# Moving the weight sums and the gate-times-up products of a Strassen-Winograd SwiGLU from GpSimd to VectorE

## The chip, the cores and the metric

The kernel runs on one core of one Trainium2 chip. The metric is the device time of one execution in microseconds (us). Five instruction engines take part: TensorE (PE: matmuls, with its weight loads shown as PEld), VectorE (DVE), ScalarE (ACT), GpSimd (POOL) and the SP queue, which only issues DMAs. Each engine runs its own instructions in their order; semaphores tie the engines to each other.

## The reference

One decoder layer in float32 over 1024 tokens and 1024 channels. The part that matters here is its feed-forward block, with 2816 hidden columns:

```python
n2 = rms_norm(h, g_ffn[i])
h = h + (jax.nn.silu(n2 @ w_ffn_gate[i]) * (n2 @ w_ffn_up[i])) @ w_ffn_down[i]
```

Ahead of it stand the two attention branches and their merge, behind it a gated per-layer embedding and the last RMSNorm.

## The kernel before

Each float32 factor of a matmul is split in two parts: `split` (lines 128 to 130) lets ScalarE cast it to the high part (L129) and VectorE subtract that from the source to get the low part (L130). `passes` (L132 to L137) then does three matmuls for each pair of blocks: high by high (L135), high by low of the moving operand (L136), low by high (L137). So the first two matmuls of a group wait for ScalarE only, and the third is the first that needs VectorE's low part.

The gate and up matmuls are done in **units**: 22 of them, alternately 256 columns of `w_ffn_gate` and the same 256 of `w_ffn_up`; two such units are called a pair. A unit's 1 MB of weights (tile `raw`, three buffers) comes by a DMA on the SP queue (L860). In `wino` a unit is a two-by-two block product done with seven products in place of eight (the Strassen-Winograd scheme). Each product is twelve matmuls of 128x512. Its left factor is a quarter of the weights or a sum of quarters, split into a tile `wl` with three buffers, so that ScalarE and VectorE prepare a product while TensorE is up to two products behind. The sums of quarters are four instructions of 128x512 for each unit on GpSimd: `s1` (L989) and L990 as soon as the weights are there, L1006 behind product 1, L1008 behind product 2.

The seven products have the order 1, 5, 2, 6, 7, 3, 4, and units overlap: products 1 and 5 of a unit, then 3 and 4 of the unit before it, then 2, 6 and 7 of the unit. The products' results are combined on VectorE by `add` (L999), three for each unit. A gate unit passes its four results through SiLU on ScalarE (L1035). An up unit multiplies its four results by those of the gate unit (`ready`, L1051): three on GpSimd (L1054), the last, straight from the bank, on VectorE (L1056). From these it forms the sums for the down matmul on VectorE (L1047) and stores all to DRAM on the SP queue (L1044). Between the units VectorE also forms sums of the down weights (`down_sums`, L1140).

The engines' instruction orders aren't written by hand: a scheduler takes the program and lays out each queue by its own estimate of times. Ahead of the units, VectorE normalizes the hidden state (L875) with a scale that TensorE broadcasts into the bank `bc` (L764) and forms the right factors `b`.

Of the kernel before, what the change touches and what calls it, by code (L numbers as in the profile page):

```python
# [14 lines left out]
ALU = mybir.AluOpType  # L15
# [36 lines left out]
def decoder_layer(ctx: ExitStack, tc: tile.TileContext, x, p, positions, g_mix, w_in, g_q_a, w_q_b,  # L52
                  g_kv_a, w_kv_b, w_br_mla, w_br_sb, w_out, g_ffn, w_ffn_gate, w_ffn_up, w_ffn_down,
                  w_ple_gate, w_ple_proj, g_ple, g_final, xT, pT, out):
    nc = tc.nc
# [72 lines left out]
    def split(h, l, src, eng=nc.vector):  # L128
        nc.scalar.copy(out=h, in_=src)  # L129
        eng.tensor_tensor(out=l, in0=src, in1=r32(h), op=ALU.subtract)  # L130

    def passes(ps, prods, first=True, last=True, **kw):  # L132
        n = len(prods)
        for i, ((ah, al), (bh, bl)) in enumerate(prods):
            nc.tensor.matmul(ps, lhsT=ah, rhs=bh, start=first and i == 0, stop=False, **kw)  # L135
            nc.tensor.matmul(ps, lhsT=ah, rhs=bl, start=False, stop=False, **kw)  # L136
            nc.tensor.matmul(ps, lhsT=al, rhs=bh, start=False, stop=last and i == n - 1, **kw)  # L137
# [17 lines left out]
    with ExitStack() as att:  # L155
# [17 lines left out]
        with ExitStack() as sb:  # L173
# [306 lines left out]
            for pr in range(HEADS // 2):  # L480
                kst, q1, q2 = cur
                oT = wp.tile([P, S], F32, name="oT", tag="oT", bufs=1)
                for a in range(2):
# [5 lines left out]
                                            op=ALU.subtract)  # L489
# [365 lines left out]
    def t_tile():  # L855
        return wk.tile([P, HALF], F32, name="t", tag="t", bufs=16)
# [127 lines left out]
    def wino(raw, order, ctile, ready):  # L984

        a11, a12, a21, a22 = [raw[:, kh * 4:kh * 4 + 4, f * P:(f + 1) * P] for f in range(2) for kh in range(2)]
        s1 = wk.tile([P, 4, P], F32, name="s1", tag="c", bufs=4)
        G = nc.gpsimd
        G.tensor_tensor(out=s1, in0=a21, in1=a22, op=ALU.add)  # L989
        G.tensor_tensor(out=a21, in0=a11, in1=a21, op=ALU.subtract)  # L990
        left = {1: a11, 2: a12, 3: a12, 4: a22, 5: s1, 6: a11, 7: a21}
        bank, s = {}, {}

        def snap(key, pt):
            s[key] = ctile()
            nc.scalar.copy(out=s[key], in_=pt)

        def add(key, pt):
            latest["add"] = nc.vector.tensor_tensor(out=s[key], in0=pt, in1=s[key], op=ALU.add).ins  # L999
            return s[key]  # L1000

        for n, i in enumerate(order):
            w = wk.tile([P, 2, 4, P], F32R, name="wl", tag="wl", bufs=3)
            split(w[:, 0], w[:, 1], left[i])
            if i == 1:
                G.tensor_tensor(out=a11, in0=s1, in1=a11, op=ALU.subtract)  # L1006
            elif i == 2:
                G.tensor_tensor(out=a12, in0=a12, in1=a11, op=ALU.subtract)  # L1008
            k = "P" if i in (1, 6, 7, 4) else "R" if i == 2 else "Q"
            first = k not in bank  # L1010
            if first:
                spec = B if k == "R" else next(firsts) if k == "Q" and order is FIRST else A
                bank[k] = ps.tile([P, HALF], F32, name="p" + k, **spec)
            pt = bank[k]
            passes(pt, [((w[:, 0, kk, :], w[:, 1, kk, :]), (Bn[i][:, 0, kk, :], Bn[i][:, 1, kk, :]))
                        for kk in range(4)], first=first, last=i in (2, 3, 4), skip_group_check=True)
            if i in (1, 6):
                snap(i, pt)
            elif i == 2:
                ready(0, 0, add(1, pt))  # L1020
            elif i == 3:
                ready(0, 1, add(6, pt))
            elif i == 4:
                ready(1, 0, None, pt)
            elif (12 - i) in s:
                ready(1, 1, add(12 - i, pt))
            else:
                snap(i, pt)
            yield

    def gate_unit(raw, order, ctile, sl):
        def ready(f, t, c, pt=None):
            if c is None:
                c = t_tile()
            nc.scalar.activation(out=c, in_=c if pt is None else pt, func=AF.Silu)  # L1035
            sl[f, t] = c

        return wino(raw, order, ctile, ready)

    def up_unit(j, raw, order, ctile, sl):  # L1040
        done = {}

        def store(i, src):
            nc.sync.dma_start(out=d_g[(7 * j + i - 1) * P:(7 * j + i) * P, :], in_=src)  # L1044

        def sub(i, dst, a, b):
            nc.vector.tensor_tensor(out=dst, in0=a, in1=b, op=ALU.subtract)  # L1047
            done[i] = dst
            store(i, dst)

        def ready(f, t, u, pt=None):  # L1051
            g = sl[f, t]
            if pt is None:
                nc.gpsimd.tensor_tensor(out=g, in0=g, in1=u, op=ALU.mult)  # L1054
            else:
                nc.vector.tensor_tensor(out=g, in0=pt, in1=g, op=ALU.mult)  # L1056
            done[f, t] = g
            if (f, t) != (0, 1):
                store({(0, 0): 1, (1, 0): 2, (1, 1): 3}[f, t], g)
            if 7 not in done and (1, 1) in done and (0, 1) in done:  # L1060
                sub(7, t_tile(), done[1, 1], done[0, 1])
            if 5 not in done and 7 in done and (0, 0) in done:
                sub(5, done[0, 1], done[0, 1], done[0, 0])
                sub(6, t_tile(), done[1, 1], done[5])
            if 4 not in done and 6 in done and (1, 0) in done:
                sub(4, t_tile(), done[1, 0], done[6])

        return wino(raw, order, ctile, ready)
# [264 lines left out]
```

## Time and profile before

| | |
|---|---|
| median of 3 runs | 1748.95 us (1746.61 to 1750.78) |
| the profiled execution | 1749.03 us, of which the profiled span is 1747.2 us |
| TensorE busy | 1665.0 us (95%), mean granted clock 0.983 |
| VectorE busy | 1115.2 us (64%) |
| ScalarE busy | 881.3 us (50%) |
| GpSimd busy | 368.6 us (21%), 389 instructions |
| the stage of the units | about 993 to 1428 us of the span |

Times in the profile are microseconds from the start of the span. "Busy" is the time in which an engine executes; a matmul of 128x512 shows as some 0.39 us busy though the next one starts after some 0.23 us, since matmuls are pipelined. An idle time has behind it, in brackets, what ended it (the releaser).

### The profile page before, as it was taken

Reading aid. Unit: us, or ns where it says so; the run is one execution under the profiler, and the core shown is the slowest. Engines: PE = TensorE matmul, PEld = TensorE weight load, DVE = VectorE, ACT = ScalarE, POOL = GpSimd, SP = SyncE. Lnnn points to the kernel's source line nnn. Section 1 sums busy time; section 2 is a strip of 40 time slices with the busy share of each in tenths; the row PEclk is TensorE's granted clock in tenths of the full one; section 3 lists DMA queues with packets and bytes.
Section 4 is the critical chain, followed back from the end, with each engine's and each line's share of the span. In section 5 each row is a group of like instructions: output and inputs, shape, how many; then the busy total and the mean of one; then the engine's idle time right before and its main releaser. Section 6 shows DMA issues by size and latency. Waiting matters only on the chain.

```text
span 1747.2 us, 22835 instructions
## 1 busy us (share of the span) xinstructions
PE 1665.0 (95%) x8100; PEld 1383.4 (79%) x8100; DVE 1115.2 (64%) x1874; ACT 881.3 (50%) x1740; POOL 368.6 (21%) x389
## 2 busy tenths in 40 slices
PE   6999999999987999998999899999999999999997
PEld 5887778777776788886789787877778778888787
DVE  6655785576766777686568745565666545656665
ACT  5255676576675776686325633333333334445412
POOL 2012220000021333331001733344344310000000
PEclk9999999999998999999999999999999999999998
DMA  5221222212223322124854423364564528665522
GB/s 175 59 69 37 61 57 65 67 60 67 85 85 127 104 68 86 59 70 157 284 201 153 145 78 129 126 216 151 187 197 163 199 88 316 193 193 183 170 81 74
DMA packets 167987, 222.10 MB, mean 127 GB/s; under 512 B 22914, under 2 KB 97666, under 8 KB 167874
## 3 DMA queue, kind: packets, MB, share of 16 engines
q1 hardware_dynamic: 161298, 200.21, 35.6%
q0 software_dynamic: 6032, 19.93, 3.3%
q8 instruction: 63, 1.03, 0.2%
q10 hardware_dynamic: 544, 0.52, 0.1%
q14 instruction: 50, 0.41, 0.1%
HBM read 151.93 MB, written 67.90 MB: 126 GB/s over the span
## 4 chain that ended last, share of the span: by engine, by line
PE 74%; DVE 10%; issue 6%; ACT 4%; DMA 3%; POOL 3%; SPq 0%; POOLq 0%; DVEq 0%; ACTq 0%
PE pt L135 5%; PE pt L136 4%; PE pt L137 4%; PE pd L135 4%; PE pd L136 4%; PE pd L137 4%; PE pP L137 4%; PE pP L135 4%; PE pP L136 4%; PE pg L135 2%; PE pg L136 2%; PE pg L137 2%; PE pb L135 2%; DVE T L433 2%; PE pb L137 2%
## 5 line engine op out<-in xcount | busy, mean ns | idle before, releaser
L135 PE MATMUL pt<-nTh,w_h 128*128 128x512 f32 (+1 forms) x480 | 191.7, 405 | 1.6 <-DVE e L436 1.1
L137 PE MATMUL pt<-nTh,w_l 128*128 128x512 f32 (+1 forms) x480 | 189.7, 401 | 1.6 <-DVE w_l L130 1.6
L136 PE MATMUL pt<-nTl,w_h 128*128 128x512 f32 (+1 forms) x480 | 190.8, 402 | 0.0
L130 DVE TENSOR_TENSOR wl<-raw,wl 128x512 fp32r<-128x512 f32 x132 | 109.4, 830 | 102.5 <-ACT wl L129 101.9
L129 ACT CAST wl<-raw 128x512 fp32r<-128x512 f32 x132 | 82.0, 622 | 127.6 <-PE pP L137 54.5
L137 PE MATMUL pP<-b,wl 128*128 128x512 f32 x352 | 137.2, 392 | 9.0 <-DVE wl L130 9.0
L135 PE MATMUL pP<-b,wl 128*128 128x512 f32 x352 | 138.0, 392 | 5.0 <-ACT wl L129 4.5
L136 PE MATMUL pP<-b,wl 128*128 128x512 f32 x352 | 137.7, 391 | 0.0
L135 PEld LDWEIGHTS pt<-nTh,w_h 128*128 128x128 f32 (+1 forms) x480 | 91.6, 191 | 22.5 <-DVE e L436 1.9
L137 PEld LDWEIGHTS pt<-nTh,w_l 128*128 128x128 f32 (+1 forms) x480 | 91.3, 190 | 20.9 <-DVE w_l L130 2.0
L136 PEld LDWEIGHTS pt<-nTl,w_h 128*128 128x128 f32 (+1 forms) x480 | 91.3, 190 | 18.4
L136 PE MATMUL pd<-drs,dls 128*128 128x512 f32 x296 | 101.4, 389 | 0.0
L137 PE MATMUL pd<-drs,dls 128*128 128x512 f32 x296 | 101.2, 389 | 0.0
L130 DVE TENSOR_TENSOR drs<-drr,drs 128x512 fp32r<-128x512 f32 x74 | 50.9, 690 | 75.3 <-ACT drs L129 75.3
L135 PE MATMUL pd<-drs,dls 128*128 128x512 f32 x296 | 98.7, 392 | 0.0
L129 ACT CAST drs<-drr 128x512 fp32r<-128x512 f32 x74 | 45.9, 623 | 99.5 <-PE pd L137 93.3
L430 DVE SCALAR_TENSOR_TENSOR e<-z,e 128x128 f32<-128x128 f32 (+3 forms) x96 | 51.2, 550 | 60.5 <-ACT e L429 60.2
L657 POOL TENSOR_SCALAR pw<-pw,st 128x128 f32<-128x128 f32 (+5 forms) x48 | 74.1, 1548 | 74.3 <-PE sp L639 22.3
L137 PEld LDWEIGHTS pP<-b,wl 128*128 128x128 f32 x352 | 66.2, 188 | 26.0 <-DVE wl L130 12.4
L455 DVE TENSOR_TENSOR tl<-tp,th 128x512 fp32r<-128x512 f32 (+1 forms) x96 | 50.9, 549 | 51.5 <-ACT th L454 51.4
L135 PEld LDWEIGHTS pP<-b,wl 128*128 128x128 f32 x352 | 66.5, 189 | 19.2 <-ACT wl L129 4.8
L136 PEld LDWEIGHTS pP<-b,wl 128*128 128x128 f32 x352 | 66.5, 189 | 13.9
(368 smaller groups left out, 4596.6 us busy)
## 6 DMA issues: line engine op xcount, KB each, us to landing
d_g<-t SPq DMA_DIRECT2D x74, 256.0 KB, 2.7
drr<-d_g SPq DMA_DIRECT2D x74, 256.0 KB, 3.1
w_raw<-w_in SPq DMA_DIRECT2D x33, 512.0 KB, 4.0
raw<-w_ffn_gate SPq DMA_DIRECT2D x11, 1024.0 KB, 6.3
raw<-w_ffn_up SPq DMA_DIRECT2D x11, 1024.0 KB, 6.0
spare<-w_ffn_down SPq DMA_DIRECT2D x44, 256.0 KB, 3.7
d_w<-spare SPq DMA_DIRECT2D x44, 256.0 KB, 6.1
drr<-d_w SPq DMA_DIRECT2D x44, 256.0 KB, 2.6
```

The lines of the kernel that those rows point to most:

```text
L129: nc.scalar.copy(out=h, in_=src)
L130: eng.tensor_tensor(out=l, in0=src, in1=r32(h), op=ALU.subtract)
L135: nc.tensor.matmul(ps, lhsT=ah, rhs=bh, start=first and i == 0, stop=False, **kw)
L136: nc.tensor.matmul(ps, lhsT=ah, rhs=bl, start=False, stop=False, **kw)
L137: nc.tensor.matmul(ps, lhsT=al, rhs=bh, start=False, stop=last and i == n - 1, **kw)
L430: nc.vector.scalar_tensor_tensor(out=e[:, 0:w], in0=z[:, 0:w], scalar=0.0, in1=e[:, 0:w], op0=ALU.max, op1=ALU.add)
L433: nc.vector.tensor_tensor_scan(out=T[:, 0:w][:, ::-1], data0=back, data1=back, initial=carry, op0=ALU.add, op1=ALU.max)
L455: nc.vector.tensor_tensor(out=tl[:, c0:], in0=tp[:, c0:], in1=r32(th[:, c0:]), op=ALU.subtract)
L657: nc.gpsimd.tensor_scalar(out=pw[:, 0:nk], in0=pw[:, 0:nk], scalar1=st[:, 6:7], scalar2=None, op0=ALU.mult)
```

## The change

The four sums of weight quarters of each unit and the three products of gate and up of each up unit are issued to VectorE in place of GpSimd. Operands, tiles and buffer counts stay as they are.

```diff
         s1 = wk.tile([P, 4, P], F32, name="s1", tag="c", bufs=4)
-        G = nc.gpsimd
+        G = nc.vector
         G.tensor_tensor(out=s1, in0=a21, in1=a22, op=ALU.add)
         G.tensor_tensor(out=a21, in0=a11, in1=a21, op=ALU.subtract)
...
             if pt is None:
-                nc.gpsimd.tensor_tensor(out=g, in0=g, in1=u, op=ALU.mult)
+                nc.vector.tensor_tensor(out=g, in0=g, in1=u, op=ALU.mult)
             else:
                 nc.vector.tensor_tensor(out=g, in0=pt, in1=g, op=ALU.mult)
```

The scheduler lays the queues out anew. The first place to look at is VectorE's queue in the middle of the stage, in the gate unit that follows an up unit (`raw_10610` is the up unit's weights, `raw_10762` those of the gate unit behind it, `raw_10901` and `raw_11045` the two units that come next). Before:

```order
L999 TENSOR_TENSOR t_10802<-pP_10771,t_10802 128x512
L1140 TENSOR_TENSOR spare_8713<-spare_8713 128x512
L130 TENSOR_TENSOR wl_10972<-raw_10610,wl_10972 128x512
L1140 TENSOR_TENSOR spare_8713<-spare_8713 128x512 x3
L130 TENSOR_TENSOR wl_10992<-raw_10762,wl_10992 128x512
L999 TENSOR_TENSOR t_10873<-pQ_10789,t_10873 128x512
L130 TENSOR_TENSOR wl_11011<-raw_10762,wl_11011 128x512
L1047 TENSOR_TENSOR t_10964<-t_10654,t_10735 128x512
L1056 TENSOR_TENSOR t_10836<-pP_10771,t_10836 128x512
L1047 TENSOR_TENSOR t_10735<-t_10735,t_10636 128x512
L130 TENSOR_TENSOR wl_11028<-raw_10762,wl_11028 128x512
```

With the change, from the split of `wl_10972` on (the two rows ahead of it, L999 and L1140, are the same):

```order
L130 TENSOR_TENSOR wl_10972<-raw_10610,wl_10972 128x512
L1054 TENSOR_TENSOR t_10654<-t_10654,t_10802 128x512
L1140 TENSOR_TENSOR spare_8713<-spare_8713 128x512 x2
L130 TENSOR_TENSOR wl_10992<-raw_10762,wl_10992 128x512
L1140 TENSOR_TENSOR spare_8713<-spare_8713 128x512
L1008 TENSOR_TENSOR raw_10762<-raw_10762 128x4x128
L999 TENSOR_TENSOR t_10873<-pQ_10789,t_10873 128x512
L130 TENSOR_TENSOR wl_11011<-raw_10762,wl_11011 128x512
L989 TENSOR_TENSOR s1_11194<-raw_11045 128x512
L1054 TENSOR_TENSOR t_10735<-t_10735,t_10873 128x512
L990 TENSOR_TENSOR raw_11045<-raw_11045 128x4x128
L1056 TENSOR_TENSOR t_10836<-pP_10771,t_10836 128x512
```

Behind the last row shown there follow L1047 (`t_10964`) and the split of `wl_11028`. Between the splits of `wl_10972` and `wl_11028` stood seven instructions and two splits; now it is eleven instructions and two splits, since two products L1054, a sum L1008 and the two first sums of unit `raw_11045` have come in and one L1047 has gone behind `wl_11028`. L989 waits for the DMA that fills `raw_11045`.

The second place is VectorE's queue ahead of the first unit, where it forms the right factors (`raw_9335` is the weights of the second unit; `pm_9583` is the column sums from which the scale of the last tokens follows, by L170, GpSimd's L171, L761 and the bank `bc_9590`). Before:

```order
L130 TENSOR_TENSOR b6_8873<-spare_8713,b6_8873 128x256 x4
L170 TENSOR_SCALAR cols_85<-pm_9583 128x2
L761 TENSOR_SCALAR acc_9069<-ident_75,cols_85 128x128 x2
L875 SCALAR_TENSOR_TENSOR t_8660<-t_8660,cols_85,bc_9590 128x256
L875 SCALAR_TENSOR_TENSOR t_8664<-t_8664,cols_85,bc_9590 128x256
```

With the change:

```order
L130 TENSOR_TENSOR b6_8873<-spare_8713,b6_8873 128x256 x4
L989 TENSOR_TENSOR s1_9483<-raw_9335 128x512
L170 TENSOR_SCALAR cols_85<-pm_9583 128x2
L990 TENSOR_TENSOR raw_9335<-raw_9335 128x4x128
L761 TENSOR_SCALAR acc_9069<-ident_75,cols_85 128x128 x2
L170 TENSOR_SCALAR cols_85<-pm_9212 128x4
L875 SCALAR_TENSOR_TENSOR t_8660<-t_8660,cols_85,bc_9590 128x256
```

L989, which waits for the DMA of the second unit's weights, and L990 now stand among the four steps that lead to the scale. On TensorE the matmul into `bc_9590` has moved behind one more group of column sums (L903) and six more matmuls of the embedding. Two splits of the right factor `b4` have moved behind the first `wl`.

## Rows read from the trace of the kernel before

**Rows 1.** The page, busy time of each engine

```profile
PE 1665.0 (95%) x8100; PEld 1383.4 (79%) x8100; DVE 1115.2 (64%) x1874; ACT 881.3 (50%) x1740; POOL 368.6 (21%) x389
```

**Rows 2.** Busy time by stretch, seven pairs of units

```profile
core 0: us, PE busy (x) PEld busy (x) DVE busy (x) ACT busy (x) POOL busy (x), PEclk, DMA share, GB/s
...
1162.26:1201.99 39.73, 38.38 (x169) 31.46 (x169) 25.50 (x33) 13.89 (x25) 16.33 (x11) 1.00 0.62 209
...
sum 276.99, PE 268.70 PEld 220.19 DVE 166.22 ACT 97.80 POOL 112.11; mean PE 38.39 PEld 31.46 DVE 23.75 ACT 13.97 POOL 16.02
```

**Rows 3.** Waits of TensorE, 1010 to 1430 (total us, times, longest)

```profile
PE pP L137 <- DVE wl L130: 9.0, 8, 1.5
...
PE pP L135 <- DVE t L999: 0.5, 1, 0.5
```

**Rows 4.** Waits of VectorE, same stretch

```profile
DVE t L1047 <- POOL t L1054: 12.0, 11, 1.2
```

**Rows 5.** Timeline of VectorE: start, us, engine, line (idle before, releaser)

```profile
1186.63 0.69 DVE L999 TENSOR_TENSOR t<-pP,t 128x512 f32<-128x512 f32 x1 [0.89 <-PE pP L137]
...
1187.84 1.78 DVE L130 TENSOR_TENSOR wl<-raw,wl 128x512 fp32r<-128x512 f32 x1
...
1192.79 1.47 DVE L130 TENSOR_TENSOR wl<-raw,wl 128x512 fp32r<-128x512 f32 x1
1195.44 0.69 DVE L1047 TENSOR_TENSOR t<-t 128x512 f32<-128x512 f32 x1 [1.19 <-POOL t L1054]
...
1197.75 1.77 DVE L130 TENSOR_TENSOR wl<-raw,wl 128x512 fp32r<-128x512 f32 x1
1199.45 0.68 DVE L1047 TENSOR_TENSOR t<-t 128x512 f32<-128x512 f32 x1
1200.05 0.68 DVE L999 TENSOR_TENSOR t<-pR,t 128x512 f32<-128x512 f32 x1
...
1201.25 0.68 DVE L130 TENSOR_TENSOR wl<-raw,wl 128x512 fp32r<-128x512 f32 x1
```

**Rows 6.** Timeline of TensorE, same pair

```profile
1201.99 0.50 PE L137 MATMUL pP<-b,wl 128*128 128x512 f32 x1 [1.34 <-DVE wl L130]
```

**Rows 7.** Timeline of GpSimd, same pair

```profile
1193.66 1.74 POOL L1054 TENSOR_TENSOR t<-t 128x512 f32<-128x512 f32 x1
1195.91 1.37 POOL L989 TENSOR_TENSOR s<-raw 128x512 f32<-128x512 f32 x1 [0.50 <-DMA raw<-w_ffn_gate]
```

**Rows 8.** Timeline of the SP queue, same pair

```profile
1189.64 0.38 SPq L860 DMA_DIRECT2D raw<-w_ffn_gate  x1
```

**Rows 9.** VectorE groups by shape, 1083.66 to 1360.65 (busy us, mean ns)

```profile
L130 DVE TENSOR_TENSOR wl<-raw,wl 128x512 fp32r<-128x512 f32 x84 | 73.8, 879 | 53.6 <-ACT wl L129 53.2
...
L1047 DVE TENSOR_TENSOR t<-t 128x512 f32<-128x512 f32 x29 | 24.9, 858 | 7.6 <-POOL t L1054 7.5
```

**Rows 10.** Tile raw, 1000 to 1380: issue to landing

```profile
DMA to landing us min/median/max: 5.2/6.1/7.8
```

**Rows 11.** Timeline of VectorE, an undisturbed stretch

```profile
1020.25 0.69 DVE L130 TENSOR_TENSOR wl<-raw,wl 128x512 fp32r<-128x512 f32 x1 [2.03 <-ACT wl L129]
1022.97 0.69 DVE L130 TENSOR_TENSOR wl<-raw,wl 128x512 fp32r<-128x512 f32 x1 [2.03 <-ACT wl L129]
```

**Rows 12.** Timeline of VectorE, start of the stage

```profile
973.14 3.23 DVE L875 SCALAR_TENSOR_TENSOR t<-t,cols,bc 128x256 f32<-128x256 f32 x8 [3.63 <-PE bc L764]
...
993.22 1.89 DVE L130 TENSOR_TENSOR wl<-raw,wl 128x512 fp32r<-128x512 f32 x3
```

**Rows 13.** Timeline of TensorE, start of the stage

```profile
972.93 0.95 PE L903 MATMUL pm<-cols,e 128*128 128x1 f32 x8
...
975.22 0.95 PE L903 MATMUL pm<-cols,e 128*128 128x1 f32 x8
...
992.95 0.80 PE L135 MATMUL pP<-b,wl 128*128 128x512 f32 x1 [4.52 <-ACT wl L129]
```

**Rows 14.** Timeline of GpSimd, start of the stage

```profile
970.74 1.28 POOL L989 TENSOR_TENSOR s<-raw 128x512 f32<-128x512 f32 x1 [1.75 <-DMA raw<-w_ffn_up]
```

## The prediction, written before the changed kernel ran

> **What bounds the kernel now.** I read the busy times first: TensorE works 95% of the span, VectorE 64%, GpSimd 21% [rows 1]. So a change on VectorE and GpSimd can only win back what TensorE loses to waits, and I look for those in the stage of the units, where all 121 instructions that move are: 22 units with four sums, and 11 up units with three products.
>
> The waits of TensorE between 1010 and 1430 us are short: nine, of which eight are for the low part of a `wl` (9.0 us together, 1.5 at most) and one of 0.5 us is for an `add` [rows 3]. The eight come once in each pair of units, at the same place. Seven pairs from stall to stall take 276.99 us, 39.57 each, at full clock throughout [rows 2]. Undisturbed, TensorE asks for a product every 2.72 us, which is the distance of two splits where VectorE only follows it [rows 11]; a pair has 14 products, 38.08 us. So a stall costs 39.57 - 38.08 = 1.49 us with all that goes with it, and eight cost 11.9 us.
>
> What is behind a stall is seen in one pair on VectorE [rows 5]. Product 7 of the gate unit is the one that TensorE waits for: it waits 1.34 us and goes on at 1201.99 [rows 6], just behind the split that starts at 1201.25. That split is late because VectorE was late three times. Two splits beside a running GpSimd instruction take 1.78 and 1.77 us, one 1.47, where 0.69 is normal. At 1195.44 VectorE has waited 1.19 us for GpSimd's product L1054, which takes 1.74 us and starts at 1193.66 [rows 7]. Over the stage this wait comes 11 times, 12.0 us [rows 4], once for each up unit. Behind the waiting L1047 in VectorE's queue stand the splits that TensorE needs.
>
> **The change part by part.** *Removed:* GpSimd's 121 instructions, so the wait for L1054 and the slow splits. Between the first and the last stall the 84 splits of weight quarters average 0.879 us and the 29 sums L1047 0.858 [rows 9]; at 0.69 that is 84 x 0.19 + 29 x 0.17 = 21 us less in seven pairs, 3.0 for each.
>
> *Added on VectorE:* in each pair eight sums and three products. No row has them on this engine; the nearest are its own 128x512 instructions with two operands, 0.68 to 0.69 us long and 0.60 apart when they stand back to back (1199.45, 1200.05) [rows 5]. Eleven x 0.69 is 7.6 us a pair. Bounds: 0.60 if all stand back to back, 0.88 if they were as slow as the splits are now. VectorE's load goes from 23.75 us a pair [rows 2] to 23.75 + 7.6 - 3.0 = 28.4, with 38.08 to do it in. On the whole it has room; the question is the narrow place ahead of the split for product 7.
>
> *The narrow place, with the new order.* I set t = 0 where the `add` at 1186.63 starts. The split is needed where TensorE began to wait, 1201.99 - 1.34 = 1200.65, t = 14.0. In the new queue L999, L1140 and the split of `wl_10972` come first: 3 x 0.60 + 0.1, t = 1.9 (before: 1187.84 + 1.78, t = 3.0 [rows 5]). That split is the last reader of a buffer of `raw`, so the next load is issued at once (L860 at 1189.64 [rows 8]). It lands 5.2 to 7.8 us later, 6.1 in the median [rows 10]: t = 8.0, between 7.1 and 9.7. Meanwhile VectorE does eight more instructions, the last split at the pace of TensorE, and comes to L989 at t = 1.9 + 4.8 = 6.7. **The new wait is here**: L989 needs the load that GpSimd waited for until now at 1195.91 [rows 7], and in VectorE's queue it holds up all that follows, 1.3 us in the median, 0.4 to 3.0. Then come L989, L1054, L990, L1056, L1047 and the split: 6 x 0.60 + 0.1 = 3.7. The split is done at t = 11.7 in the median, 13.4 behind the slowest load. Needed is 14.0. So there are 2.3 us to spare, 0.6 at worst, and the stall goes. In the other half of the pair L990 and a split follow L989 at once, with no product and no down sum around them, so it has more room. The next to be late is nothing in the unit: TensorE runs at its 2.72.
>
> The Trainium skill says why the splits are slow (SBUF — State Buffer, section "Who interferes with whom"): a VectorE instruction with two inputs in SBUF and a GpSimd instruction that reads SBUF exclude each other for a whole instruction. The 1.78 us beside GpSimd's instruction [rows 5, 7] agree. By that rule no slow split is left in the stage; were they to stay as slow as now, the load would be 31.4 us a pair, which changes neither the sum nor the range.
>
> *The start of the stage.* Here VectorE is without a pause from 973.14 to the first `wl` at 993.22 [rows 12]. The scale's matmul moves on TensorE behind one group of column sums and six matmuls, which is the stretch from 972.93 to 975.22: 2.3 us [rows 13]. The load that L989 waits for lands at 970.74 [rows 14]; L989, L170, GpSimd's power and L761 need some 3 us from there, 973.7, so it is in time for that slot but by one microsecond only. Two splits go behind, -1.2. The first low part is then 1.1 us later. TensorE first does six matmuls that need only high parts, from 992.95 on, when the buffers of `wl` come free [rows 13]; 6 x 2.72/12 = 1.4 us cover the 1.1 but for VectorE's own 0.69. So 0 to +0.5; if the load came 3 us later, +3. I take +0.4.
>
> *Sum* against the profiled execution of 1749.03 us (span 1747.2 and 1.8 around it; the median of the runs is 1748.95, so the same): -11.9 + 0.4 = -11.5, **1737.5 us**. The single wait of 0.5 us for an `add` I leave in. Best case: that goes too and the start costs nothing, 1736.6, less some 2 us by which single runs lie below the median: 1734.5.
>
> **The rivals.**
>
> *The loads hold up part of the units.* For: GpSimd waits for L989's load in nearly all units, and VectorE now would. Against: the 0.6 us that are left behind the slowest load. It decides from 14.0 - 3.7 - 1.9 = 8.4 us from issue to landing, against 7.8 at most now. If half the gain is lost so, or the start costs its 3 us and some pairs stall: -6, 1743.
>
> *Slower: the loads hold up every pair by more than now.* The same wait with a load of over 8.4 + 1.5 = 9.9 us; 0.2% (3.5 us over ten pairs) is lost from 10.3 us on, at 11 us it is 10 x 1.1 = +11, 1760. For: a load's time isn't VectorE's to choose, and stores and down weights share its DMA engines. Against: no load of the stage came near it [rows 10].
>
> *VectorE saturates.* From t = 0 to the split it now has seventeen instructions, 10.3 us at 0.60, which with the wait of 1.3 makes 11.7 of 14.0. It would be late if each took 0.74 (with the median load; 17 x 0.74 + 1.3 = 13.9) for a reason that isn't GpSimd. Then the stall stays: 1749, no change. Against: the row at 0.60, and 2.72 us of pause between splits elsewhere [rows 11]. The Trainium skill would have it this way round (Perfetto Trace Analysis, section "Optimizing Scalar/DVE Operations"): where VectorE is saturated, giving work to other engines, even GpSimd, may pay. By that rule taking it back costs; 64% busy doesn't speak for it.
>
> *The wait is not what costs.* If the slow split and L1054 are not on the way to the stall but ScalarE's cast is, nothing changes: 1749. The releaser in [rows 6] speaks against it.
>
> **How the numbers follow.** Forecast 0.66 (1734.5 to 1741); part of the gain lost 0.14 (1741 to 1745.5); slower 0.09; VectorE saturated 0.06 and another cause of the stall 0.05, both without a change. What a measurement tells from no change is about 0.2%, 3.5 us. The range takes the first two: 1734.5 to 1745.5, 0.80. Faster 0.80, same 0.11, slower 0.09.
>
> **What would show it.** In the changed kernel's trace: GpSimd without any instruction between 1010 and 1420 us; the splits of `wl` at 0.69 us in the mean; pairs of 38.1 us in place of 39.6; no wait of TensorE for a `wl`; VectorE some 1.3 us idle ahead of L989, with the load as releaser. The prediction is wrong if TensorE waits behind such an L989, if the first product of the stage starts later than 993, or if pairs at 38.1 us don't show in the total.

## The result, and the profile after

The changed kernel takes 1739.85 us (1738.38 to 1741.08) against 1749.37 (1746.61 to 1750.78) before; the ratio is 0.9946, with a 95% interval of 0.9932 to 0.9960. That is 9.5 us less by the medians, and 7.0 to 11.9 by the interval. Forecast were 11.5 less, 1737.5, between 1734.5 and 1745.5.

The page of the changed kernel, busy time of each engine, and the waits of TensorE and of VectorE between 1009 and 1418 us (total us, times, longest):

```profile
PE 1666.0 (96%) x8100; PEld 1385.5 (80%) x8100; DVE 1153.4 (66%) x1995; ACT 881.9 (51%) x1740; POOL 180.8 (10%) x268
```

```profile
PE pd L135 <- ACT dwl L129: 0.7, 1, 0.7
PE pP L137 <- DVE wl L130: 0.6, 2, 0.3
```

```profile
DVE s L989 <- DMA raw<-w_ffn_up: 14.9, 10, 3.1
DVE s L989 <- DMA raw<-w_ffn_gate: 10.7, 9, 1.8
```

Against [rows 1], GpSimd has lost 121 instructions and 188 us, and VectorE has gained the 121 but only 38 us. TensorE's waits for a `wl` are down from 9.0 us in eight to 0.6 in two, and the one for an `add` is gone [rows 3]. VectorE no longer waits for GpSimd [rows 4]; in its place stands the wait of L989 for its load, 25.6 us in 19 (1.35 each).

Seven pairs by stretch, from one L1056 to the same one seven pairs later, and VectorE's groups by shape there (busy us, mean ns):

```profile
1078.30:1346.80 268.50, 267.75 (x1178) 220.23 (x1177) 184.99 (x293) 97.52 (x168) 0.00 (x0) 1.00 0.55 178
```

```profile
L130 DVE TENSOR_TENSOR wl<-raw,wl 128x512 fp32r<-128x512 f32 x84 | 57.8, 688 | 36.3 <-ACT wl L129 36.0
L1047 DVE TENSOR_TENSOR t<-t 128x512 f32<-128x512 f32 x27 | 18.4, 683 | 0.0
```

A pair takes 268.50 / 7 = 38.36 us, where it took 39.57 [rows 2]; GpSimd does nothing; VectorE is busy 184.99 / 7 = 26.4 us in each; splits take 0.688 us in place of 0.879 and L1047 0.683 in place of 0.858 [rows 9].

The pair that the prediction worked through, on VectorE and then TensorE. Columns: start, us, engine, line, operands, idle before and its releaser.

```profile
1183.20 0.69 DVE L999 TENSOR_TENSOR t<-pP,t 128x512 f32<-128x512 f32 x1 [0.89 <-PE pP L137]
...
1184.41 0.69 DVE L130 TENSOR_TENSOR wl<-raw,wl 128x512 fp32r<-128x512 f32 x1
...
1191.79 0.69 DVE L989 TENSOR_TENSOR s<-raw 128x512 f32<-128x512 f32 x1 [1.62 <-DMA raw<-w_ffn_gate]
...
1194.80 0.69 DVE L130 TENSOR_TENSOR wl<-raw,wl 128x512 fp32r<-128x512 f32 x1
1195.40 0.69 DVE L1047 TENSOR_TENSOR t<-t 128x512 f32<-128x512 f32 x1
1196.00 0.68 DVE L999 TENSOR_TENSOR t<-pR,t 128x512 f32<-128x512 f32 x1
1196.60 0.68 DVE L130 TENSOR_TENSOR wl<-raw,wl 128x512 fp32r<-128x512 f32 x1
```

```profile
1197.34 0.50 PE L137 MATMUL pP<-b,wl 128*128 128x512 f32 x1
```

With t = 0 at the `add` at 1183.20, the split beside nobody takes 0.69 us, the load lands at t = 8.6, and the split of `wl_11028` (product 7) starts at t = 11.6. But TensorE's matmul at 1197.34 comes 0.06 us behind the end of the *next* split, at 1197.28, t = 14.1. That is the split that TensorE needs here, and it is only just in time: TensorE idles 0.12 us ahead of this matmul, too short to be marked. TensorE's queue, read again, says why: product 1 of the next unit goes ahead of product 7, before the change and after it. Three groups of it in their order (bank, right factor, left factor):

```
pP_10914<-b6_8873,wl_11011
pP_11058<-b1_8870,wl_11054
pP_10914<-b7_8874,wl_11028
```

The trace bears this order out. By the kernel, ScalarE copies product 1 out of its bank (L996), while product 7 goes to VectorE's `add`. What follows the group with the matmul at 1197.34 is the copy, and the `add` comes one group later. Before the change the same copy starts at 1204.59, behind the group with the matmul at 1201.99. With the change:

```profile
1199.96 0.59 ACT L996 COPY t<-pP 128x512 f32<-128x512 f32 x1 [1.61 <-PE pP L137]
```

```profile
1203.13 0.69 DVE L999 TENSOR_TENSOR t<-pP,t 128x512 f32<-128x512 f32 x1 [1.34 <-PE pP L137]
```

So the wait in [rows 6] is that of product 1 for the split of `wl_11054`, which is the one at 1201.25 in [rows 5], and not of product 7 for `wl_11028`, which had been ready since 1199.5.

### The profile page after: what moved, and what is told of

Read it like the earlier page. It is cut to its first block, busy times and chain, and to the rows that moved or that the text cites. A ratio compares the mean times of both kernels' runs of the same rounds, so it can differ in the third digit from the quotient of the medians.

```text
span 1736.6 us, 22714 instructions
## 1 busy us (share of the span) xinstructions
PE 1666.0 (96%) x8100; PEld 1385.5 (80%) x8100; DVE 1153.4 (66%) x1995; ACT 881.9 (51%) x1740; POOL 180.8 (10%) x268
## 4 chain that ended last, share of the span: by engine, by line
PE 78%; DVE 7%; issue 5%; DMA 4%; ACT 4%; POOL 1%; SPq 0%; POOLq 0%; DVEq 0%; ACTq 0%
PE pt L135 5%; PE pt L136 5%; PE pt L137 5%; PE pP L137 4%; PE pP L135 4%; PE pP L136 4%; PE pd L135 4%; PE pd L136 4%; PE pd L137 4%; PE pQ L136 2%; PE pQ L135 2%; PE pQ L137 2%; PE pg L135 2%; PE pg L136 2%; PE pg L137 2%
## 5 line engine op out<-in xcount | busy, mean ns | idle before, releaser
L130 DVE TENSOR_TENSOR wl<-raw,wl 128x512 fp32r<-128x512 f32 x132 | 90.8, 688 | 72.4 <-ACT wl L129 72.0
L137 PEld LDWEIGHTS pP<-b,wl 128*128 128x128 f32 x352 | 66.5, 189 | 16.7 <-DVE wl L130 3.0
L135 PEld LDWEIGHTS pP<-b,wl 128*128 128x128 f32 x352 | 66.9, 190 | 16.1 <-ACT wl L129 2.4
L171 POOL TENSOR_TENSOR r<-r,cols 128x2 f32<-128x2 f32 (+1 forms) x3 | 2.4, 802 | 726.4 <-DVE r L170 726.4
```

Source lines behind the costliest of these rows:

```text
L171: nc.gpsimd.tensor_tensor(out=out_r, in0=out_r, in1=mhalf.broadcast_to([P, n]), op=ALU.pow)
```

## The experiments

All are timed against the kernel before, which took 1748.26 us in the runs beside e1 to e4 and 1747.69 in those beside e0 and e5 to e7; the ratios go against these. The diffs show each edit against the changed kernel. The theory: a pair is late by what VectorE needs from the `add` to the split of `wl_11054`, and slow instructions beside GpSimd, the wait for L1054, the load's wait and VectorE's own instructions all add up on this way. Rival A: the wait for L1054 alone makes the stall. Rival B: the slow instructions alone do. For the start of the stage: the change costs time there, or the clock does by chance.

**Products alone (e1).**

```diff
-        G = nc.vector
+        G = nc.gpsimd
```

> Only the 33 products L1054 move to VectorE; the 88 sums stay on GpSimd. Theory (stall = slow splits plus the wait of L1047, added up on VectorE's way to the split for product 7): in the pair at 1186.63 the way loses the 1.1 us of the split beside L1054 and the wait of 1.19, gains two products of 0.60, and keeps the slow instructions beside L1008, L989 and L990. The split is done at 15.3 - 1.1 - 1.2 + 1.2 = 14.2, needed is 14.0. So 0.2 to 0.3 us of each stall stay, TensorE's waits for wl fall from 9.0 to about 2 us, and the time is 1739.5 (1738 to 1742), with no cost at the start of the stage because its queues stay as before. Rival A (the wait for L1054 alone makes the stall): all of it goes, 1737. Rival B (the slow splits alone; the products are 3 of 11 GpSimd instructions in a pair): a quarter goes, 1746.

Measured 1740.41, ratio 0.9955 (0.9942 to 0.9969): 7.9 us less. VectorE beside GpSimd, and the stall that is left:

```profile
1194.01 0.69 DVE L1056 TENSOR_TENSOR t<-pP,t 128x512 f32<-128x512 f32 x1
1194.62 1.45 DVE L1047 TENSOR_TENSOR t<-t 128x512 f32<-128x512 f32 x1
1196.00 1.77 DVE L130 TENSOR_TENSOR wl<-raw,wl 128x512 fp32r<-128x512 f32 x1
```

```profile
1194.24 1.29 POOL L989 TENSOR_TENSOR s<-raw 128x512 f32<-128x512 f32 x1 [2.06 <-DMA raw<-w_ffn_gate]
1195.60 1.61 POOL L990 TENSOR_TENSOR raw<-raw 128x512 f32<-128x512 f32 x1
```

```profile
1200.23 0.50 PE L137 MATMUL pP<-b,wl 128*128 128x512 f32 x1 [0.36 <-DVE wl L130]
```

The L1047 that meets GpSimd's L989 takes 1.45 us, the split that meets its L990 1.77. Each starts while the GpSimd instruction runs and ends some 0.55 us behind its end: L1047 at 1196.07 behind 1195.53, the split at 1197.77 behind 1197.21. So this is no slower pace: VectorE's instruction stands still until the other has ended. In the six traces that have GpSimd instructions in the stage (1010 to 1430 us), 244 VectorE instructions of 128x512 with both operands in SBUF start while one of GpSimd runs, and 225 of them end 0.53 to 0.57 us behind it. Of the other 19, fourteen meet only its last 0.13 us or less, four start within 0.05 us of it, and one meets two in a row. The 195 that start first take 0.69 us at most, and GpSimd's is the longer one then, as L990 above (1.61 us, against 1.29 for L989).

TensorE's waits for a `wl` are 2.6 us in five, where the theory had about 2. A's 1737 lies just below the interval, and A left no stall; B's 1746 is far above.

**Sums alone (e2).**

```diff
-                nc.vector.tensor_tensor(out=g, in0=g, in1=u, op=ALU.mult)
+                nc.gpsimd.tensor_tensor(out=g, in0=g, in1=u, op=ALU.mult)
```

> Only the 88 sums move to VectorE; the products L1054 stay on GpSimd. Theory: the split for product 7 is done at about 12.2 (slow splits beside L1054 only, L989 held to 9.1 by its load), needed 14.0, so the stalls go although L1047 may still wait for L1054; the start has the same queues as with the whole change and costs its 2.6 us: 1740 (1738.5 to 1742). Rival A (the wait for L1054 alone makes the stall): the stalls stay, 1749 + 2.6 = 1751. Rival B (slow splits alone): three quarters go, 1743.

Measured 1742.46, ratio 0.9974 (0.9962 to 0.9987): 4.5 us less by the ratio, 5.8 by the medians, and above the expected range. TensorE's waits for a `wl` are 4.9 us in seven, and they were expected to go.

```profile
1184.60 1.77 DVE L130 TENSOR_TENSOR wl<-raw,wl 128x512 fp32r<-128x512 f32 x1
...
1192.47 0.69 DVE L989 TENSOR_TENSOR s<-raw 128x512 f32<-128x512 f32 x1 [1.52 <-DMA raw<-w_ffn_gate]
...
1195.01 0.68 DVE L130 TENSOR_TENSOR wl<-raw,wl 128x512 fp32r<-128x512 f32 x1
1195.61 0.68 DVE L1047 TENSOR_TENSOR t<-t 128x512 f32<-128x512 f32 x1
1196.21 0.68 DVE L999 TENSOR_TENSOR t<-pR,t 128x512 f32<-128x512 f32 x1
1196.81 0.68 DVE L1047 TENSOR_TENSOR t<-t 128x512 f32<-128x512 f32 x1
1197.41 0.68 DVE L130 TENSOR_TENSOR wl<-raw,wl 128x512 fp32r<-128x512 f32 x1
```

The load landed where expected (t = 9.1), and the wait for L1054 has shrunk to 2.4 us in two, since GpSimd is free when a product comes. The expectation went wrong in the split: its 12.2 is the end of the split of `wl_11028` (1195.69, t = 12.3), but the one that counts ends at t = 14.7. Rival A (1751) is out, B is nearest by the time, but not by the trace: one slow split, the one that releases the load, and the load's wait behind it make the stall.

**L989 and L990 back on GpSimd (e3).**

```diff
-        G.tensor_tensor(out=s1, in0=a21, in1=a22, op=ALU.add)
-        G.tensor_tensor(out=a21, in0=a11, in1=a21, op=ALU.subtract)
+        nc.gpsimd.tensor_tensor(out=s1, in0=a21, in1=a22, op=ALU.add)
+        nc.gpsimd.tensor_tensor(out=a21, in0=a11, in1=a21, op=ALU.subtract)
```

> L989 and L990, which wait for the load, stay on GpSimd; L1006, L1008 and L1054 are on VectorE. TensorE's queue is then the same as before the change. Theory: the split for product 7 is done at 15.3 - 1.1 - 1.2 - 0.8 + 1.2 + 0.6 = 14.0, so the stalls go or stay at 0.1 to 0.2 us, slow splits stay only beside two GpSimd instructions of a unit, VectorE never waits for a raw, and the start costs nothing: 1737.5 (1736 to 1740), some 2 us below the whole change. Rival (the 2.6 us at the start are chance of the clock and not of L989 in VectorE's queue): no better than the whole change, 1739 to 1741, with the granted clock at the half level from 981 us on here too.

Measured 1738.59, ratio 0.9946 (0.9934 to 0.9958), the same as the whole change. The load's wait is gone from VectorE, but L1047 and a split, 1.62 and 1.78 us long beside the two sums, take its place: 2.6 us of stalls in five, where 0.1 to 0.2 us each at most were expected. In the profiles the stage is 2.5 us longer than with the whole change and the start 2.3 shorter (table below); but against the repetition of the change (e0, below) the start is only 0.4 shorter, so how the times come out equal isn't shown. The time lies between the 1737.5 of the theory and the 1739 of the rival and decides neither.

**GpSimd beside VectorE, with nobody waiting for it (e6).** The whole change, with useless sums on GpSimd.

```diff
+    scr = wk.tile([P, 4, P], F32, name="scr", bufs=1)
+    SIDE = (1, 5, 2, 6, 4)
...
             split(w[:, 0], w[:, 1], left[i])
+            if i in SIDE and order is ORDER:
+                nc.gpsimd.tensor_tensor(out=scr, in0=w[:, 0], in1=w[:, 0], op=ALU.add)
```

> The whole change, and from the fourth unit on GpSimd does one sum of 128x512 beside the splits of five products of each unit, into a scratch tile that nobody reads and nobody on VectorE waits for: 95 instructions, ten for each pair where the kernel before had eleven. Theory (GpSimd beside VectorE slows it, without any wait between the two): the splits beside them take 1.4 to 1.8 us in place of 0.69, VectorE's busy time rises by 70 to 100 us, the load is released 1.1 later and the split that TensorE needs ends at least 2.2 us later than without; it had no spare, so the stalls come back larger than before the change: 1740 + 8 x 2.2 = 1758 (1750 to 1775). Rival A (only the wait of VectorE for GpSimd's products cost): 1740, no stall, splits 0.69.

Measured 1747.80, ratio 1.0003 (0.9993 to 1.0013): the whole gain is gone, though VectorE waits for no GpSimd instruction. The time is below the expected 1750 to 1775. VectorE's busy time is 1209.4 us, 56 more than with the whole change, where 70 to 100 were expected. Its groups by shape between 1011 and 1420 us, with this kernel's own line numbers (L1012 is the sum L1008, L1001 is `add`):

```profile
L130 DVE TENSOR_TENSOR wl<-raw,wl 128x512 fp32r<-128x512 f32 x125 | 106.8, 855 | 53.2 <-ACT wl L129 53.0
...
L1012 DVE TENSOR_TENSOR raw<-raw 128x512 f32<-128x512 f32 x19 | 26.4, 1390 | 0.3
...
L1001 DVE TENSOR_TENSOR t<-pQ,t 128x512 f32<-128x512 f32 x21 | 14.3, 680 | 2.1 <-PE pQ L137 2.1
L1001 DVE TENSOR_TENSOR t<-pP,t 128x512 f32<-128x512 f32 x20 | 13.8, 692 | 18.7 <-PE pP L137 18.7
L1001 DVE TENSOR_TENSOR t<-pR,t 128x512 f32<-128x512 f32 x19 | 13.0, 685 | 3.7 <-PE pR L137 3.7
```

```profile
1202.23 0.50 PE L137 MATMUL pP<-b,wl 128*128 128x512 f32 x1 [1.70 <-DVE wl L130]
```

The instructions with both operands in SBUF are slowed, the sum L1012 to 1.39 us in the mean. The `add`, with one operand in a bank, isn't: in the six traces 97 instructions with such an operand start while a GpSimd instruction runs, and none takes more than 0.693 us. There are six stalls of 1.2 to 1.7 us, 9.7 together. Rival A is out. So is another, that the scratch sums hold up the buffers of `wl` that they read: none of ScalarE's waits ahead of a cast in the stage is for GpSimd. The stall is smaller than the 2.2 expected since the first slow instructions of a pair use up the time that L989 would have waited for its load.

**Is there anything to spare (e7)?** The whole change and two useless products for each up unit but the first. In the pair below both stand ahead of the split that TensorE needs and one L1047 has gone behind it, so one instruction more has to be done first.

```diff
                 nc.vector.tensor_tensor(out=g, in0=g, in1=u, op=ALU.mult)
+                if j and (f, t) == (0, 1):
+                    for _ in range(2):
+                        nc.vector.tensor_tensor(out=scr, in0=g, in1=u, op=ALU.mult)
```

> The whole change and two further products on VectorE behind the second L1054 of each up unit, into a scratch tile that nobody reads; the scheduler puts one of them and, net, one instruction more (0.60 us) between the wait for the load and the splits that TensorE needs. The prediction gives 2.3 us of spare there: no change, 1740. Theory after the trace of the change (TensorE takes product 1 of the next unit ahead of product 7; the split that it needs is the later one, done at 14.1 where 14.0 is needed, so nothing is to spare): 0.6 us of stall in most of the eight pairs, TensorE's waits for wl from 0.6 to 4 or 5 us, 1744 (1742.5 to 1746).

Measured 1740.83, ratio 0.9959 (0.9945 to 0.9974). The time is nearer to the 1740 of the prediction and below the 1742.5 to 1746 of the theory, but the interval of the ratio holds both 1740 and 1744 (0.9946 and 0.9969 of the 1749.37 that the change was timed against), so it cannot tell them apart. The trace can: TensorE waits for a `wl` again, 3.5 us in six, five of them at this place.

```profile
1202.96 0.69 DVE L130 TENSOR_TENSOR wl<-raw,wl 128x512 fp32r<-128x512 f32 x1
```

```profile
1203.70 0.50 PE L137 MATMUL pP<-b,wl 128*128 128x512 f32 x1 [0.50 <-DVE wl L130]
```

This split ends at t = 14.47, with the change alone at 14.08, and the load landed 0.23 us earlier here: together 0.62 us, one instruction. The stall is 0.50 us where it was 0.12, so there was nothing like 2.3 us to spare.

**The same pair in all kernels.** From the start of the `add` (t = 0) to the end of the split of `wl_11054`, and TensorE's wait as the trace marks it:

| kernel | split ends at t | TensorE waits |
|---|---|---|
| e6, whole change and GpSimd beside it | 15.66 | 1.70 |
| e5, first three units only (below) | 15.36 | 1.39 |
| before [rows 5, 6] | 15.30 | 1.34 |
| e2, sums alone | 14.70 | 0.75 |
| e3, L989 and L990 on GpSimd | 14.53 | 0.57 |
| e7, two more products | 14.47 | 0.50 |
| e1, products alone | 14.32 | 0.36 |
| the change | 14.08 | none marked |
| e4, first three units as before (below) | 13.97 | none marked |
| e0, the change again (below) | 13.93 | none marked |

Wherever a wait is marked it is the split's time less 13.96, to 0.01 us, and so it is for the stalls at this place in the other pairs of these traces. From the `add` on TensorE goes at its own pace and loses only what this split is late. Slow instructions, a wait for GpSimd, a wait for a load and plain instructions count alike; no run takes away the wait for GpSimd alone, so its own share is added up and not measured.

**The start of the stage.** Three runs: the change again; the first three units' sums as before; and only these changed.

```diff
-        G = nc.vector
+        G = nc.gpsimd if order is FIRST else nc.vector
```

(e4; in e5 the two engines are swapped, and the products stay on GpSimd.)

> The whole change, a second time, for the start of the stage. Theory (the start costs 2 to 3 us because L989 and L990 stand among the steps that lead to the scale): 74 to 75 us again from GpSimd's first power L171 at the end of the out projection to the third L999, where the kernel before has 72.0; 1740 (1738 to 1742). Rival (that clock fall was chance): about 72, and 1737.5.

> The whole change from the fourth unit on; the first three units' sums stay on GpSimd, so that the queues up to the first unit are as before. Theory (the start's 2.6 us come from L989 and L990 among the four steps that lead to the scale, and from TensorE's order that follows from it): the stage gains its 11.9 or a little less and the start costs nothing, 1737.3 (1736 to 1739). Rival (the start's cost is chance): 1739.9 as with the whole change, or the clock falls at 981 us here too.

> Only the sums of the first three units are on VectorE; everything else is as before the change. Theory: the start costs 2 to 2.6 us (first L171 to third L999 74 to 74.6 in place of 72.0), the stalls of the stage stay at 9 us: 1749 + 2.3 = 1751 (1749.5 to 1752.5). Rival (the start costs nothing, chance): 72 us there and 1749.

Measured: e0 1738.64, ratio 0.9946 (0.9932 to 0.9960); e4 1737.53, 0.9938 (0.9927 to 0.9950); e5 1748.88, 1.0003 (0.9993 to 1.0014). The start, from GpSimd's first power L171 to the third `add` of the stage, and the stage, from there to the last L1056:

| kernel | first L171 at | start, us | stage, us |
|---|---|---|---|
| before | 939.40 | 72.00 | 416.79 |
| e1 | 941.47 | 72.08 | 409.28 |
| e3 | 936.74 | 72.37 | 408.94 |
| e4 | 937.11 | 72.87 | 406.29 |
| the change | 936.95 | 74.64 | 406.47 |
| e0, the change again | 939.51 | 72.76 | 406.00 |
| e2 | 936.25 | 73.82 | 411.90 |
| e5 | 936.68 | 73.50 | 415.42 |
| e6 | 939.21 | 73.61 | 417.04 |
| e7 | 942.83 | 73.66 | 409.96 |

The first column lies ahead of all that the change touches and differs by up to 6.6 us from run to run, so whole spans of single executions are not to be compared. The upper four have TensorE's start in the old order, the lower six in the new one. They average 72.3 and 73.7. Whether those 1.3 us are the order's isn't shown, since the granted clock differs too. Counted from the first L171, it is back from the lower level at 56.4 (before), 56.7 (e1), 57.3 (e3) and 58.1 us (e4) in the old order, and at 58.4 (e0), 59.7 (e5), 59.8 (e6), 60.0 (e7), 60.4 (e2) and 60.6 us (the change) in the new one, and but for e4 and e0, nearly alike in this (72.87 in the old order, 72.76 in the new one), the start is longer the later that is, over both orders. On VectorE the new order does cost: the first split of a `wl` starts 1.0 us later (54.8 against 53.8 from the first L171), and the third ends 2.8 us later (58.5 against 55.7), in all six against all four.

The change and its repetition have the same order and differ by 1.9 us. The stretches of the change and of its repetition (TensorE, its loads, VectorE, ScalarE, GpSimd busy; granted clock, DMA share, GB/s):

```profile
980.00:985.00 5.00, 5.00 (x19) 4.19 (x18) 5.00 (x10) 4.66 (x11) 0.00 (x0) 0.54 0.14 52
985.00:990.00 5.00, 5.00 (x24) 5.00 (x25) 5.00 (x13) 3.15 (x6) 0.00 (x0) 0.50 0.65 198
990.00:995.00 5.00, 3.28 (x8) 2.09 (x9) 5.00 (x10) 1.67 (x3) 3.06 (x1) 0.50 0.85 327
```

```profile
980.00:985.00 5.00, 5.00 (x36) 4.57 (x35) 5.00 (x12) 5.00 (x14) 0.00 (x0) 1.00 0.28 105
985.00:990.00 5.00, 4.10 (x28) 3.85 (x26) 5.00 (x13) 5.00 (x11) 0.00 (x0) 0.77 0.59 172
990.00:995.00 5.00, 2.75 (x7) 1.46 (x7) 5.00 (x12) 2.02 (x4) 0.49 (x1) 0.50 0.98 305
```

In the one the granted clock falls 43.5 us after the first L171 (980.4) and is at the lower level while TensorE still has the embedding's matmuls to do (19 matmuls in a slice); in the other it falls 48.2 us after it (987.7), when they are nearly done and TensorE would wait anyway. So the repetition is nearer to the rival, chance, than to the 74 to 75 expected. e5's ratio says +0.5 us (-1.2 to +2.4), where 2.3 were expected; its time is below the expected range, but the interval holds both 0 and 2.3, so it doesn't decide. e4 came out as the theory had it and has the lowest median of all, but its interval overlaps that of the change: whether it is better stays open.

## Why the prediction was right, and where its steps were not

*The bound and the cause* held. TensorE lost to waits for a low part, and VectorE was late by slow instructions and by the wait for L1054. The experiments show both at work: without the wait but with GpSimd beside it (e6) the gain is gone, and moving the products alone (e1, 7.5 us less in the stage) or the sums alone (e2, 4.9) gives part each. The wait's own share is worked out, not measured: each run that takes it away takes slow instructions away too. The parts do not add up (12.4 against 10.3 for both), because under 13.96 us nothing more is won.

*The step that failed* is "the split for product 7, done at t = 11.7, needed at 14.0, 2.3 us to spare". The need was read rightly from [rows 6], but from the split of another product: TensorE takes product 1 of the next unit first, and its split stands three instructions further back in VectorE's queue: t = 11.7 + 3 x 0.60 = 13.5 with the median load at 8.0, and 14.1 with this pair's at 8.6. So the forecast came near the truth by luck: the stall ends where the spare ends, and the spare was about nothing in this pair and not 2.3 us. One sign of being wrong that the prediction named did come, though small: TensorE waits behind such an L989 in two pairs, 0.3 us each. The others did not: the first product of the stage starts at 989.8 us, not later than 993, and the shorter pairs show in the total. With 0.5 us to spare in the median, the rival "the loads hold up part of the units" deserved more than 0.14: it decides from 14.0 - 5.5 - 1.9 = 6.6 us from issue to landing, and not from 8.4, and the loads of [rows 10] go up to 7.8.

*The sizes.* The stage gives 10.3 us (416.79 - 406.47) in place of 11.9: the marked waits fall by 8.4 and 0.5, and the rest is what goes with a stall unmarked. Some 0.3 us in each pair are left (38.36, forecast 38.08), as the split is on time and no earlier. The start took 2.6 us more in the profiled execution in place of 0.4, 0.8 in the repetition. This is inside the prediction's 0 to 3, but the 3 were for a late load, and no load was late: 1.9 of the 2.6 are the difference to the repetition, which goes with the granted clock (above). The first low part came 1.0 us later, forecast 1.1. The sum for the profiled span is -10.3 + 2.6 and 0.5 less behind the stage, and 2.4 less ahead of the change's first effect, where it alters nothing: 1736.6 against 1747.2.

*VectorE's load* is 26.4 us a pair, 28.4 forecast. The added instructions stand mostly back to back, 0.60 each and not 0.69 (1.0 less), and the splits of `s1`, at 1.0 us before, were left out of the relief. The load's wait of L989 was 1.35 us in the mean, 1.3 forecast.

*The slow instructions.* Two operands in SBUF are slowed beside GpSimd, 1.39 us in the mean for L1012 of e6, and an `add` with one operand in a bank is not, 0.680 to 0.692. The Trainium skill states both halves (SBUF — State Buffer, section "Who interferes with whom"): a VectorE instruction with two inputs in SBUF contends with a GpSimd instruction that reads SBUF, and one with at most one such input does not. The trace agrees, and the ends 0.55 us behind GpSimd's bear out the "for a whole instruction" of the prediction. The 1.78 us that it gave as the row for it stand beside an earlier L1054 (1187.40 to 1189.06), which [rows 7] doesn't show.

The prediction's other rule from the Trainium skill (Perfetto Trace Analysis, section "Optimizing Scalar/DVE Operations") has VectorE's saturation as its condition. No run here comes to that: VectorE was busy 64% before, 66% with the change and 69% in e6. The prediction left out what the same section of the Trainium skill adds, that moving work between VectorE and GpSimd might not help.

## What to carry to other kernels

A small helper on GpSimd is not free for VectorE, even when nobody waits for it: five sums beside each unit's splits ate the whole gain. What counts is who starts first and where the operands lie: behind a running GpSimd instruction a VectorE instruction with both operands in SBUF stood still until that one's end, and one with an operand in a bank didn't. When a stall's slack is worked out, take the names of the tiles from the waiting engine's queue: two splits of a `wl` stood close together here, and the argument took the wrong one. And where two causes feed one late instruction, removing either gives more than its share, since the gain ends where the lateness ends.

## Not expected of the hardware

The granted clock of TensorE fell to the lower level at 980.4 us in the profiled execution of the change, 43.5 us after the first L171, with TensorE 5.00 of 5.00 us busy in the slice before and in that slice. In the same kernel's repetition it fell 48.2 us after it, and in the other eight kernels 47.0 to 50.2. What TensorE did before in the two was the same order of matmuls. This goes with the 1.9 us between their starts, more than the 1.3 by which the two orders' means differ. Why it fell early in the one stays open.
